# First expert pair in a row, the ranks' order ahead of it, and weight units on a 512-byte start

## The chip, the core and the metric

The kernel runs on one core of a Trainium2 chip. The metric is the device time of one execution in microseconds (us), the median of several runs. The core has a matrix engine (TensorE, PE in the rows), a vector engine (VectorE, DVE), a scalar engine (ScalarE, ACT), GpSimd (POOL) and SyncE (SP), which here issues nearly all transfers from HBM into the on-chip memory (SBUF). Sixteen DMA engines carry each transfer out. Matrix products land in PSUM banks, of which this kernel uses four as `mm` and four as `ax`.

## The reference

One layer of a backbone over 256 tokens of 1,024 features: an attention and gating part, and then a mixture of experts. All of it is in float32.

```python
x = layer_norm(ALPHA * x + g1 * mix_x, ln1_g, ln1_b)
logits = t @ router_w + router_b                 # t: modulated layer norm of x, 256 x 1024
top_vals, top_idx = lax.top_k(logits, 4)         # 4 of 32 experts for each token
combine = sum(one_hot(top_idx, 32) * softmax(top_vals))
for each expert e:
    gu = t @ w_gu[e] + b_gu[e]                   # 1024 x 2048
    gate, lin = minimum(gu[:, :1024], 7), clip(gu[:, 1024:], -7, 7)
    y = ((lin + 1) * gate * sigmoid(1.702 * gate)) @ w_down[e] + b_down[e]
    acc += combine[:, e] * y
x = layer_norm(ALPHA * x + g2 * acc, ln2_g, ln2_b)
```

An expert's weights are 12 MiB, all 32 together 384 MiB.

## The kernel before

**Units and the stream.** SBUF is cut into 26 units of 8 KiB in each of the 128 partitions (1 MiB each, pool `uni`). Weights come as pieces that fill one unit (L193 to L232): 38 for the front part, then per expert 8 for gate and up and 4 for down. `pump` issues the next piece of the list into a free unit, and `done` frees a unit after its last product and pumps one piece more. The code is recorded by hand in the order in which each engine runs it; SP's queue is in order too, so a transfer that waits for its unit holds back those behind it.

**Groups.** The first group is the fixed pair of experts 0 and 1, whose pieces can be issued early. Then come twelve groups of one, two or four experts, sorted by how many tokens each expert got: counting tokens (`rank_counts`) gives ranks and the permutation `perm`, `rank_order` turns it into the list of expert numbers `ordi`, and SP loads a number from it (L213) before it can issue that expert's first piece. So no piece of the second group can be issued before `ordi` is written; `streams` puts all those pieces on the list.

**One group** (`group`, L1199): four steps of gate and up (gate 0, up 0, gate 1, up 1; two halves each, the bias first, L894, then L1114), with the activation on VectorE and ScalarE between, a transpose of the result (`h_T`, L1145), and two down products (L1160). Between them, at named places ("in0" inside the first step, "gu0" behind it, and so on), hooks run other work on the same engines. For the first pair these are the counts (in0), the order, the tables by rank and the stream (gu0), the tables' lookup (in1), `finish_G`, the first weighting transpose and the next group's one-hot tables (gu1), and the next group's gather (gu2: L888 and the weighting transpose L951). Two units are taken from the pair's freed ones for other use: `take_late` after the first step (table and bias storage, with four small loads, L997), `t2_unit` after the third.

**Before the pair** the second half of the tokens is routed (L795 to L804), its one-hot table written (L875) and gathered (L888) into the banks `gb0`; `modulate_cols` (L776) scales the gathered columns, the first half on VectorE, the second on ScalarE, and `gate` computes the four weights per token.

Of the kernel before, what the change touches and what calls it, by code (L numbers as in the profile page):

```python
# [18 lines left out]
P = 128  # L19
# [5 lines left out]
NE = 32  # L25
# [40 lines left out]
def hybrid_layer_kernel(  # L66
# [12 lines left out]
    router_w = router_w[0]  # L79
    w_gu, b_gu, w_dn, b_dn = exp_w_gu, exp_b_gu[0], exp_w_down, exp_b_down[0]  # L80

    cst = ctx.enter_context(tc.tile_pool(name="cst", bufs=1))
    uni = ctx.enter_context(tc.tile_pool(name="uni", bufs=1))
    mo = ctx.enter_context(tc.tile_pool(name="mo", bufs=2))
    sm = ctx.enter_context(tc.tile_pool(name="sm", bufs=4))
    pm = ctx.enter_context(tc.tile_pool(name="pm", bufs=4, space=bass.MemoryType.PSUM))
# [72 lines left out]
        return bass.AP(tensor=src.tensor, offset=src.offset, ap=[[0, parts], [1, n]])  # L159


    ident = cst.tile([P, P], F32, name="ident")
    make_identity(nc, ident)
    mhalf = cst.tile([P, 1], F32, name="mhalf")
    G.memset(mhalf, -0.5)


# [604 lines left out]
        for j in range(4):  # L772
            G.partition_broadcast(late_v["g2"][:, j * 256:(j + 1) * 256], late["rows"][32 * j:32 * j + 1, :])

    def modulate_cols(dst, bank, hh, act_only=False):
        for k in range(4):  # L776
            kk = hh * 4 + k
            src = bank[:, k * P:(k + 1) * P]
            if act_only or hh:
                S.activation(dst[:, kk, :], src, AF.Identity, scale=sc2[:, kk:kk + 1], bias=sh2[:, kk:kk + 1])  # L780
            else:
                V.tensor_scalar(dst[:, kk, :], src, sc2[:, kk:kk + 1], sh2[:, kk:kk + 1],
                                op0=ALU.mult, op1=ALU.add)
# [32 lines left out]
    def route_T(t, hh):  # L816
        tT = late["xg"][:, t * 1024:t * 1024 + 1024].rearrange("p (k n) -> p k n", n=P)
        pt = ax_bank()
        for k in range(4):
            PE.transpose(pt[:, k * P:(k + 1) * P], late["tMv"][:, t, (hh * 4 + k) * P:(hh * 4 + k + 1) * P], ident)  # L820
        return lambda: modulate_cols(tT, pt, hh, t == 0)

    def route_mm(t):
        tT = late["xg"][:, t * 1024:t * 1024 + 1024].rearrange("p (k n) -> p k n", n=P)
# [66 lines left out]
    def gu_bias(part, j, sel):  # L891
# [2 lines left out]
        PE.matmul(b, sel[r, :], bgu[r, :], start=True, stop=False)  # L894
        return b

    oh0 = mo.tile([P, TT, 2, 64], F32, tag="oh", bufs=1, name="oh0")
    gb0 = [mm_bank() for _ in range(2)]
    ln_second(0)
# [21 lines left out]
    top(1)  # L921
    choose(1)
    positions(1)
    one_hot(oh0, pm1[:, :, 0:2], 1)
    for hh in range(2):
        gather_mm(gb0[hh], oh0, 1, hh)
    tM, xg_u = late["tMv"], late["xg"]
    for u in (late["l1"], gg_u):
        release(u)
# [28 lines left out]
    def gather(oh, banks=None):  # L958
        xg_i[0] ^= 1
        xg = xg_u[:, xg_i[0] * 1024:xg_i[0] * 1024 + 1024].rearrange("p (k n) -> p k n", k=KT)  # L960
        for hh in range(2):
            if banks:
                b = banks[hh]
            else:
                b = ax_bank()
                for t in range(TT):
                    gather_mm(b, oh, t, hh)
            modulate_cols(xg, b, hh)
        return xg

    xg0 = gather(oh0, gb0)
    msk4 = mo.tile([P, TT, P], F32, tag="sT", name="msk4").rearrange("p t n -> p (t n)")[:, 0:P].bitcast(BF16)
    msk4 = msk4.rearrange("p (t r e) -> p t r e", t=TT, r=4)
    V.tensor_copy(msk4, mskb[:, :, None, :].to_broadcast([P, TT, 4, NE]))
    for t in range(TT):
        gate(t)
    cur = [xg0, None]
    ohg0 = weigh(oh0, comb[:, :, 0:2])


    cc = cst.tile([P, 1], F32, name="cc")
    kr = cst.tile([P, NE], F32, name="kr")
    kc = cst.tile([P, 1], F32, name="kc")
    rank = cst.tile([P, 1], F32, name="rank")
    perm = cst.tile([P, NE], F32, name="perm")
    ordi = cst.tile([1, NE], I32, name="ordi")

    late_v = {}

# [14 lines left out]
                          start=True, stop=True)  # L1004
        V.tensor_copy(dst, b[:, 0:2 * TT * NE].rearrange("p (a t e) -> p a t e", a=2, t=TT))

    pc4 = t2_own[1].rearrange("p (a t r e) -> p a t r e", a=2, t=TT, r=4)
    V.tensor_copy(pc4[:, 0], pm1[:, :, None, :].to_broadcast([P, TT, 4, NE]))
    V.tensor_copy(pc4[:, 1], comb[:, :, None, :].to_broadcast([P, TT, 4, NE]))

    def rank_counts():
        b = ax_bank()
        for t in range(TT):
            PE.matmul(b[:, 0:NE], ones_b, mskb[:, t, :], start=t == 0, stop=t == TT - 1)
        for t in range(TT):
            PE.matmul(b[:, 64:65], msk4[:, t].rearrange("p r e -> p (r e)"), ones_b[:, 0:1],
                      start=t == 0, stop=t == TT - 1)
        V.tensor_copy(cc, b[:, 64:65])
        V.scalar_tensor_tensor(kr, b[:, 0:NE], 32.0, keyb, op0=ALU.mult, op1=ALU.add)
        V.scalar_tensor_tensor(kc, cc, 32.0, keyc, op0=ALU.mult, op1=ALU.add)  # L1020
        V.tensor_scalar(kr, kr, kc, None, op0=ALU.is_gt)
        V.reduce_sum(rank, kr, axis=AX.X)
        V.tensor_scalar(perm, iota0[:, 0:NE], rank, None, op0=ALU.is_equal)

    def rank_order():
        b = ax_bank()
        PE.matmul(b[0:1, 0:NE], ecol, perm[0:NE, :], start=True, stop=True)
        V.tensor_copy(ordi, b[0:1, 0:NE])
        b = ax_bank()
        for a in range(2):  # L1030
            for t in range(TT):
                PE.transpose(b[:, (a * TT + t) * P:(a * TT + t + 1) * P],
                             pc4[:, a, t].rearrange("p r e -> p (r e)"), ident)
        V.tensor_copy(late_v["pcT"], b.rearrange("p (a n) -> p a n", a=2))
# [70 lines left out]
    def gu_step(n, gid, part, j, xg, sel, between=None):  # L1105
        w = P // n
        b = gu_first.pop(0) if gu_first else gu_bias(part, j, sel)
        for half in range(2):
            if half and between:
                between()  # L1110
            first = gid == 0 and part == j == half == 0
            for a, k in ([(a, k) for a in range(n) for k in range(4)] if first else
                         [(a, k) for k in range(4) for a in range(n)]):
                PE.matmul(b[a * w:(a + 1) * w, :], xg[:, half * 4 + k, a * w:(a + 1) * w],  # L1114
                          weights((gid, part, j, half, a))[:, k, :], start=False, stop=half == 1 and k == 3)
                if first and k == 3:
                    done((gid, part, j, half, a))
            if not first:
                for a in range(n):
                    done((gid, part, j, half, a), (gid, part, half, a) != (0, 0, 1, 1))  # L1120
        if (gid, part) == (0, 0):
            (t2_unit if j else take_late)()
        return b

    def swiglu_gate(b):
# [64 lines left out]
    def group(n, gid, cur, sel, hooks):  # L1190
        xg = cur[0]

        def hook(name):
            for f in hooks.get(name, ()):
                f()

        b = gu_step(n, gid, 0, 0, xg, sel, lambda: hook("in0"))
        if gid == 0:
            hook("gu0")  # L1199
        g_0 = swiglu_gate(b)  # L1200
        if gid != 0:
            hook("gu0")
        b = gu_step(n, gid, 1, 0, xg, sel, lambda: hook("in1"))
        l_0 = swiglu_lin(b, g_0)
        hook("gu1")
        b = gu_step(n, gid, 0, 1, xg, sel, lambda: hook("in2"))
        g_1 = swiglu_gate(b)
        h0 = h_T(l_0)
        hook("gu2")
        b = gu_step(n, gid, 1, 1, xg, sel, lambda: hook("in3"))  # L1210
        l_1 = swiglu_lin(b, g_1)
        yb = [mm_bank() for _ in range(2)]
        if gid == len(groups) - 1:
            hs = (h0, h_T(l_1))
            zst2.extend(sm.tile([P, 2, 6], F32, tag="zst", bufs=2, name=nm("zst")) for _ in range(TT))
            down(n, gid, hs, 0, yb[0], last=True)
            ys = [scaled(yb[0], 0)]
            scatter(ys, cur[1], [0])
            down(n, gid, hs, 1, yb[1], last=True)
            y = scaled(yb[1], 1)  # L1220
            for t in range(TT):
                PE.matmul(sums[t], cur[1][:, t, :], y, start=False, stop=True)
                V.bn_stats(zst2[t][:, 1, :], sums[t])
            return None
        hs = [h0]
        down(n, gid, hs, 0, yb[0], 0, 4)
        hs.append(h_T(l_1))
        down(n, gid, hs, 0, yb[0], 4)
        ys = [scaled(yb[0], 0)]
        down(n, gid, hs, 1, yb[1])  # L1230
        for h in hs:
            t2_free(h)
        ys.append(scaled(yb[1], 1))
        return lambda: scatter(ys, cur[1])

    plan = list(PLAN)
# [26 lines left out]
    for gi, rk in enumerate(groups):  # L1263
        n = 2 if rk is None else len(rk)
        nxt = groups[gi + 1] if gi + 1 < len(groups) else None
        box = {}
        hooks = {k: [] for k in ("in0", "gu0", "in1", "gu1", "in2", "gu2", "in3")}

        def prep():
            a, m = nxt[0], len(nxt)  # L1270
# [14 lines left out]
            cur[1] = weigh_T(ohg0)  # L1285

        if gi == 0:
            hooks["in0"] += [rank_counts]
            hooks["gu0"] += [rank_order, streams]
            hooks["gu1"] += [finish_G]  # L1290
            hooks["in1"] += [lambda: by_rank(late_v["pcr"], perm[0:NE, :])]
            hooks["gu1"] += [first_T, prep]
        else:
            if nxt:
                hooks["gu0"] += [prep]
# [10 lines left out]
            S.dma_start(l2_u[0:1, 0:D], ln2_g)  # L1306
            S.dma_start(l2_u[0:1, D:2 * D], ln2_b)
        if nxt:
            hooks["gu2"] += [fetch]
        if gi == 4:  # L1310
            def spread(js):
                for j in js:
# [104 lines left out]
```

## Time and profile before

| | us |
|---|---|
| median of 3 runs | 1139.0 |
| lowest, highest | 1137.99, 1139.81 |
| the profiled execution's own time | 1136.04 |
| its span (first to last instruction) | 1134.3 |
| TensorE busy | 997.4 (88%) |
| VectorE busy | 306.0 (27%) |
| DMA queue of SP: share of 16 engines | 96.4% |

The span begins with the front part; the first expert pair runs from about 198 to 252 us, and the twelve other groups fill the rest. A busy TensorE is not one at its peak: its products are pipelined. The 450 MB that SP's queue moves are nearly all weights. A row of stretches gives busy times, the granted TensorE clock (1.00 is the upper level, 2.4 GHz) and the rate in GB/s; a timeline row gives a start, a duration, what ran, and in brackets how long the engine had been idle and what ended that.

### The profile page before, as it was taken

The numbers are of one execution on the slowest core, as the hardware profiler recorded it, in microseconds if no ns is written. First come the engines' busy times: TensorE is split into PE (matmuls) and PEld (weight loads), VectorE is DVE, ScalarE is ACT, GpSimd is POOL, SyncE is SP. The second block draws the span as 40 slices with busy tenths as digits, with TensorE's granted clock in tenths as the row PEclk, the third lists the DMA queues.
The fourth block names the chain that finished last, engine by engine and source line by source line (L and its number), as shares of the span: only waits on it lengthen the run. The fifth ranks groups of instructions, "written<-read, shape, count | busy, mean of one in ns | idle before, by whom it ended". The sixth has DMA issues, their size and how long they took to land. (4 is left out here: it accounts for less than half of the span.)

```text
span 1134.3 us, 13253 instructions
## 1 busy us (share of the span) xinstructions
PE 997.4 (88%) x5140; PEld 421.6 (37%) x5140; DVE 306.0 (27%) x621; ACT 132.8 (12%) x286; POOL 27.7 (2%) x57
## 2 busy tenths in 40 slices
PE   5999897999779999986799999987799999977765
PEld 4897465333214433321253434222134343421111
DVE  6596765314103121210121212111021211201003
ACT  4343342100100101110010101000001010100000
POOL 2000300000000000000000000000000000000000
PEclk9999898999989999988999999988899999999988
DMA  9998599799999999999989999999999999999995
GB/s 381 421 396 325 229 360 366 307 386 422 420 421 421 421 420 421 422 420 421 420 343 422 421 421 420 421 422 421 421 422 420 420 422 420 421 422 421 421 420 190
DMA packets 66296, 451.32 MB, mean 398 GB/s; under 512 B 8627, under 2 KB 8883, under 8 KB 12725
## 3 DMA queue, kind: packets, MB, share of 16 engines
q1 hardware_dynamic: 66082, 450.03, 96.4%
q8 instruction: 42, 0.69, 0.2%
q10 hardware_dynamic: 148, 0.40, 0.1%
q14 instruction: 24, 0.20, 0.0%
HBM read 449.36 MB, written 1.05 MB: 397 GB/s over the span
## 5 line engine op out<-in xcount | busy, mean ns | idle before, releaser
L1114 PE MATMUL mm<-w,xg 128*32 128x512 f32 (+2 forms) x2048 | 424.9, 620 | 42.7 <-DMA w<-in_exp_w_gu_dram 42.7
L1160 PE MATMUL mm<-w,t 128*32 128x512 f32 (+2 forms) x1024 | 235.2, 645 | 52.2 <-DMA w<-in_exp_w_down_dram 43.6
L1114 PEld LDWEIGHTS mm<-w,xg 128*32 128x32 f32 (+2 forms) x2048 | 127.9, 130 | 325.6 <-issue 242.4
L1160 PEld LDWEIGHTS mm<-w,t 128*32 128x32 f32 (+2 forms) x1024 | 67.4, 133 | 207.9 <-issue 109.9
L1187 DVE TENSOR_TENSOR t<-mm,late 128x512 f32<-128x512 f32 x26 | 18.0, 692 | 263.0 <-PE mm L1160 263.0
L1130 ACT ACTIVATE t<-t 128x512 f32<-128x512 f32 x26 | 16.4, 630 | 583.0 <-DVE t L1128 583.0
L1137 DVE TENSOR_SCALAR t<-mm 128x512 f32<-128x512 f32 x26 | 18.0, 692 | 222.7 <-PE mm L1114 222.7
L1128 DVE TENSOR_SCALAR t<-mm 128x512 f32<-128x512 f32 x26 | 18.0, 691 | 215.4 <-PE mm L1114 215.4
L894 PE MATMUL mm<-bgu,sel 32*128 32x512 f32 x104 | 58.4, 641 | 4.0 <-PEq L1240 4.0
L1170 PE MATMUL ax<-t,sT 128*128 128x512 f32 x100 | 46.3, 605 | 0.8 <-DVE t L1187 0.8
L888 PE MATMUL ax<-oh,tM 128*128 128x128 f32 x384 | 44.8, 275 | 0.0
L888 PEld LDWEIGHTS ax<-oh,tM 128*128 128x128 f32 x384 | 43.8, 192 | 0.0
L1149 ACT COPY t<-ax 128x512 f32<-128x512 f32 x26 | 15.0, 576 | 190.6 <-PE ax L1145 190.6
L245 POOL TENSOR_TENSOR rs<-rs,mhalf 128x1 f32<-128x1 f32 x12 | 9.5, 797 | 1047.4 <-DVE mv L257 919.5
L1172 DVE TENSOR_TENSOR xin<-xin,ax 128x512 f32<-128x512 f32 x50 | 33.2, 684 | 5.2 <-PE ax L1170 4.8
L1170 PEld LDWEIGHTS ax<-t,sT 128*128 128x128 f32 x100 | 18.0, 189 | 29.2 <-issue 24.6
L894 PEld LDWEIGHTS mm<-bgu,sel 32*128 32x128 f32 x104 | 15.3, 183 | 34.3 <-issue 24.5
L780 ACT ACTIVATE xg<-ax,sh,sc 128x128 f32<-128x128 f32 x60 | 22.4, 457 | 32.3 <-PE ax L888 26.5
L414 DVE TENSOR_TENSOR wlo<-w,whi 128x1024 fp32r<-128x1024 f32 x20 | 23.7, 1223 | 3.1 <-ACT whi L411 3.1
L411 ACT CAST whi<-w 128x1024 fp32r<-128x1024 f32 x20 | 20.1, 1047 | 9.5 <-PE mm L446 9.5
L1145 PEld LDWEIGHTS ax<-ident,t 128*128 128x128 f32 x104 | 11.2, 141 | 21.8 <-issue 16.8
L525 DVE SCALAR_TENSOR_TENSOR accB<-w,front,accB 128x2048 f32<-128x2048 f32 x8 | 18.8, 2348 | 0.0
(261 smaller groups left out, 717.8 us busy)
## 6 DMA issues: line engine op xcount, KB each, us to landing
w<-in_exp_w_gu_dram SPq DMA_DIRECT2D x256, 1024.0 KB, 19.8
w<-in_exp_w_down_dram SPq DMA_DIRECT2D x124, 1024.0 KB, 19.8
w<-in_w_front_dram SPq DMA_DIRECT2D x38, 1024.0 KB, 10.7
w<-in_exp_w_down_dram SPq DMA_DIRECT2D x4, 512.0 KB, 16.1
w<-in_exp_w_down_dram SPq DMA_DIRECT2D x8, 256.0 KB, 6.9
T<-in_rpb_dram SPq DMA_DIRECT2D x2, 768.0 KB
xin<-in_x_dram SPq DMA_DIRECT2D x2, 512.0 KB
cin<-in_ctx_dram SPq DMA_DIRECT2D x2, 512.0 KB, 6.4
```

What stands on the lines that cost most here:

```text
L411: S.copy(av[:, k], w[:, k])
L414: V.tensor_tensor(bv[:, k], w[:, k], av[:, k].bitcast(F32), op=ALU.subtract)
L525: V.scalar_tensor_tensor(accB_u, w[:, 0, :], sT[:, k, 0:1], accB_u, op0=ALU.mult, op1=ALU.add)
L780: S.activation(dst[:, kk, :], src, AF.Identity, scale=sc2[:, kk:kk + 1], bias=sh2[:, kk:kk + 1])
L888: PE.matmul(bank[:, k * P:(k + 1) * P], late["tMv"][:, t, (hh * 4 + k) * P:(hh * 4 + k + 1) * P], oh[:, t].rearrange("p n w -> p (n w)"), ...
L894: PE.matmul(b, sel[r, :], bgu[r, :], start=True, stop=False)
L1114: PE.matmul(b[a * w:(a + 1) * w, :], xg[:, half * 4 + k, a * w:(a + 1) * w], weights((gid, part, j, half, a))[:, k, :], start=False, stop= ...
L1128: V.tensor_scalar_min(gtile, b, 7.0)
L1137: V.tensor_scalar(lt, b, 7.0, -7.0, op0=ALU.min, op1=ALU.max)
L1160: PE.matmul(bank[a * w:(a + 1) * w, :], hs[kk // 4][:, kk % 4 * P + a * w:kk % 4 * P + (a + 1) * w], weights((gid, nn, r0, a))[:, k, :], s ...
L1170: PE.matmul(b, st[:, t, :], ys[nn], start=True, stop=True)
L1172: V.tensor_tensor(sl, sl, b, op=ALU.add)
```

## The change

It does four things.

- A new pool `pad` with one tile of 128 bytes stands first, and the units' pool `uni` in front of the constants' pool `cst`. In the built program the units begin at byte 512 of each partition instead of 9,888. All else about them is the same.
- `rank_counts` is split. Its products stand ahead of the second half of the gather before the pair, its VectorE steps (`rank_perm`) behind that gather, and ScalarE modulates the first half of those columns, VectorE the second.
- `rank_order` is split too. The part that gives `ordi`, and the stream, move to the hook "in0" inside the first step. The tables by rank become `ranks_T`.
- Three hooks are added in the down part of a group: "dn0" inside the first down product, "dn1" between the two, "dn2" behind the second. In the first pair all the other work moves there, and `take_late` goes to the end of the fourth step.

```diff
+    pad = ctx.enter_context(tc.tile_pool(name="pad", bufs=1))
+    uni = ctx.enter_context(tc.tile_pool(name="uni", bufs=1))
     cst = ctx.enter_context(tc.tile_pool(name="cst", bufs=1))
-    uni = ctx.enter_context(tc.tile_pool(name="uni", bufs=1))
...
+    mhalf = pad.tile([P, 32], F32, name="mhalf")[:, 0:1]
...
-    mhalf = cst.tile([P, 1], F32, name="mhalf")
...
+    def rank_counts():
+        msk4 = mo.tile([P, TT, P], F32, tag="sT", name="msk4").rearrange("p t n -> p (t n)")[:, 0:P].bitcast(BF16)
+        msk4 = msk4.rearrange("p (t r e) -> p t r e", t=TT, r=4)
+        V.tensor_copy(msk4, mskb[:, :, None, :].to_broadcast([P, TT, 4, NE]))
+        b = ax_bank()
+        for t in range(TT):
+            PE.matmul(b[:, 0:NE], ones_b, mskb[:, t, :], start=t == 0, stop=t == TT - 1)
+        for t in range(TT):
+            PE.matmul(b[:, 64:65], msk4[:, t].rearrange("p r e -> p (r e)"), ones_b[:, 0:1],
+                      start=t == 0, stop=t == TT - 1)
+        return b
+
+    def rank_perm(b):
+        V.tensor_copy(cc, b[:, 64:65])
+        V.scalar_tensor_tensor(kr, b[:, 0:NE], 32.0, keyb, op0=ALU.mult, op1=ALU.add)
+        V.scalar_tensor_tensor(kc, cc, 32.0, keyc, op0=ALU.mult, op1=ALU.add)
+        V.tensor_scalar(kr, kr, kc, None, op0=ALU.is_gt)
+        V.reduce_sum(rank, kr, axis=AX.X)
+        V.tensor_scalar(perm, iota0[:, 0:NE], rank, None, op0=ALU.is_equal)
...
     positions(1)
+    counts = rank_counts()
     one_hot(oh0, pm1[:, :, 0:2], 1)
     for hh in range(2):
         gather_mm(gb0[hh], oh0, 1, hh)
+    rank_perm(counts)
...
-            modulate_cols(xg, b, hh)
+            modulate_cols(xg, b, hh, not hh if banks else None)
...
     def rank_order():
         b = ax_bank()
         PE.matmul(b[0:1, 0:NE], ecol, perm[0:NE, :], start=True, stop=True)
         V.tensor_copy(ordi, b[0:1, 0:NE])
+
+    def ranks_T():
+        pc4 = t2("pc4").rearrange("p (a t r e) -> p a t r e", a=2, t=TT, r=4)
+        V.tensor_copy(pc4[:, 0], pm1[:, :, None, :].to_broadcast([P, TT, 4, NE]))
+        V.tensor_copy(pc4[:, 1], comb[:, :, None, :].to_broadcast([P, TT, 4, NE]))
         b = ax_bank()
...
-                    done((gid, part, j, half, a), (gid, part, half, a) != (0, 0, 1, 1))
-        if (gid, part) == (0, 0):
-            (t2_unit if j else take_late)()
+                    done((gid, part, j, half, a), (gid, j, half, a) != (0, 1, 1, 1))
+        if (gid, j) == (0, 1):
+            (take_late if part else t2_unit)()
...
         down(n, gid, hs, 0, yb[0], 0, 4)
         hs.append(h_T(l_1))
+        hook("dn0")
         down(n, gid, hs, 0, yb[0], 4)
         ys = [scaled(yb[0], 0)]
+        hook("dn1")
         down(n, gid, hs, 1, yb[1])
...
         ys.append(scaled(yb[1], 1))
+        hook("dn2")
...
-            hooks["in0"] += [rank_counts]
-            hooks["gu0"] += [rank_order, streams]
-            hooks["gu1"] += [finish_G]
-            hooks["in1"] += [lambda: by_rank(late_v["pcr"], perm[0:NE, :])]
-            hooks["gu1"] += [first_T, prep]
+            hooks["in0"] += [rank_order, streams]
+            hooks["dn0"] += [finish_G, ranks_T]
+            hooks["dn1"] += [lambda: by_rank(late_v["pcr"], perm[0:NE, :]), prep]
+            hooks["dn2"] += [first_T]
...
-            hooks["gu2"] += [fetch]
+            hooks["gu2" if gi else "dn2"] += [fetch]
```

TensorE, first step of the pair, before: the last half of the gather (L888), the first half of the step for either expert (L1114), the counts (L1014, L1016), two of the eight products of the second half, the order (L1027) and the tables' transposes (L1032).

```order
L888 MATMUL mm_1601<-oh_1599,tM_1473 128x128 x4
L1114 MATMUL mm_1685<-w_1117,xg_1474 64x512 x4
L1114 MATMUL mm_1685<-w_1214,xg_1474 64x512 x4
...
L1014 MATMUL ax_1829<-mskb,one_b 128x32
...
L1016 MATMUL ax_1829<-one_b,msk_1791 128x1
L1114 MATMUL mm_1685<-w_1224,xg_1474 64x512
L1114 MATMUL mm_1685<-w_1285,xg_1474 64x512
...
L1027 MATMUL ax_1853<-perm,ecol 1x32
L1032 MATMUL ax_1856<-ident,t_1_76 128x128 x4
```

The same place after:

```order
L912 MATMUL ax_1779<-mskb,one_b 128x32
...
L914 MATMUL ax_1779<-one_b,msk_1777 128x1
L890 MATMUL mm_1609<-oh_1608,tM_1476 128x128 x4
L890 MATMUL mm_1610<-oh_1608,tM_1476 128x128 x4
L1122 MATMUL mm_1694<-w_1120,xg_1477 64x512 x4
L1122 MATMUL mm_1694<-w_1217,xg_1477 64x512 x4
L1030 MATMUL ax_1841<-perm,ecol 1x32
L1122 MATMUL mm_1694<-w_1227,xg_1477 64x512
L1122 MATMUL mm_1694<-w_1288,xg_1477 64x512
```

The counts stand ahead of the gather, the order behind the first half of the step, and the tables' transposes are gone from here.

SP, the queue behind the pair's last piece, before: that piece, the four loads of `take_late`, the first expert number and its first piece.

```order
L225 DMA w_1823<-in_exp_w_down_dram 128x2048
L997 DMA late_1848<-in_exp_b_down_dram 32x256 x4
L213 TENSOR_LOAD ordi
L213 ISA x2
L218 ISA
L218 DMA w_1862<-in_exp_w_gu_dram 128x2048
```

After:

```order
L227 DMA w_1835<-in_exp_w_down_dram 128x2048
L215 TENSOR_LOAD ordi
L215 ISA x2
L220 ISA
L220 DMA w_1844<-in_exp_w_gu_dram 128x2048
```

The number is loaded straight behind the last piece; the four small loads stand thirteen pieces further on.

TensorE, from the fourth step's bias to the second group's first bias, after (before, the gather L888, its weighting transpose L951 and the tables' lookup stood ahead of the fourth step):

```order
L896 MATMUL mm_1957<-bgu,sel_1600 128x512
...
L1153 MATMUL ax_2002<-ident,t_249_1947 128x128 x4
L1040 MATMUL ax_2014<-ident,t_1_79 128x128 x4
...
L1024 MATMUL ax_2033<-perm,late_1981 128x32 x4
...
L982 MATMUL ax_2072<-ident,ohg_1825 128x128 x2
L890 MATMUL ax_2077<-oh_2039,tM_1476 128x128 x8
L890 MATMUL ax_2090<-oh_2039,tM_1476 128x128 x8
L982 MATMUL ax_2103<-ident,ohg_2044 128x128 x2
L896 MATMUL mm_2108<-bgu,sel_2042 128x512
```

What stood between the steps now stands between and behind the down products.

## Rows read from the trace of the kernel before

**Rows 1.** Page, costliest groups: busy us, mean ns, idle before it, releaser.

```profile
L1160 PE MATMUL mm<-w,t 128*32 128x512 f32 (+2 forms) x1024 | 235.2, 645 | 52.2 <-DMA w<-in_exp_w_down_dram 43.6
```

**Rows 2.** Stretches: us; PE, PEld, DVE, ACT, POOL busy; clock, DMA share, GB/s.

```profile
200.00:245.00 45.00, 44.33 (x221) 17.97 (x221) 13.60 (x39) 6.21 (x15) 1.82 (x4) 1.00 0.81 327
...
300.00:560.00 260.00, 224.28 (x1016) 79.14 (x1015) 42.47 (x95) 15.18 (x32) 0.00 (x0) 0.95 1.01 421
```

**Rows 3.** The same view in short stretches, around the two holes.

```profile
209.00:210.00 1.00, 1.00 (x8) 0.35 (x6) 0.56 (x1) 0.36 (x1) 0.00 (x0) 1.00 0.35 49
210.00:211.00 1.00, 1.00 (x8) 0.36 (x6) 0.00 (x0) 0.99 (x2) 0.00 (x0) 1.00 0.47 115
211.00:212.00 1.00, 1.00 (x7) 0.25 (x3) 0.41 (x1) 0.56 (x1) 0.00 (x0) 1.00 0.94 393
230.00:235.00 5.00, 5.00 (x25) 1.66 (x26) 0.00 (x0) 0.81 (x3) 0.00 (x0) 1.00 0.71 267
235.00:240.00 5.00, 5.00 (x26) 1.70 (x24) 1.39 (x2) 0.00 (x0) 0.00 (x0) 1.00 0.89 369
```

**Rows 4.** Timeline of SP's queue, 197 to 210 us: start, duration, transfer.

```profile
201.99 0.33 SPq L225 DMA_DIRECT2D w<-in_exp_w_down_dram  x1
...
203.76 1.72 SPq L997 DMA_DIRECT2D late<-in_exp_b_down_dram  x4
...
208.92 0.38 SPq L218 DMA_DIRECT2D w<-in_exp_w_gu_dram  x1
```

**Rows 5.** Timeline of TensorE in the first pair: start, duration, products.

```profile
203.67 0.21 PE L1014 MATMUL ax<-mskb,one_b 128*128 128x32 bf16 x2
...
207.44 0.21 PE L1027 MATMUL ax<-perm,ecol 32*1 32x32 f32 x2
207.58 0.66 PE L1032 MATMUL ax<-ident,t 128*128 128x128 f32 x4
...
216.34 0.44 PE L951 MATMUL ax<-ident,ohg 128*128 128x128 f32 x2
...
225.27 3.74 PE L888 MATMUL ax<-oh,tM 128*128 128x128 f32 x32
228.84 0.38 PE L951 MATMUL ax<-ident,ohg 128*128 128x128 f32 x2
...
240.66 0.66 PE L1145 MATMUL ax<-ident,t 128*128 128x128 f32 x4
241.99 10.52 PE L1160 MATMUL mm<-w,t 128*64 128x512 f32 x48 [0.67 <-ACT t L1149]
252.44 1.12 PE L894 MATMUL mm<-bgu,sel 32*128 32x512 f32 x2
253.49 3.64 PE L1114 MATMUL mm<-w,xg 128*32 128x512 f32 x32
```

**Rows 6.** Timeline of VectorE, 198 to 208 us: the copy, first and last rank step, cast.

```profile
198.81 0.22 DVE L974 COPY msk<-mskb 128x256 bf16<-128x256 bf16 x1
...
203.96 0.16 DVE L1018 COPY cc<-ax 128x1 f32<-128x1 f32 x1 [0.18 <-PE ax L1016]
...
205.15 0.59 DVE L1023 TENSOR_SCALAR perm<-iotas,rank 128x32 f32<-128x32 f32 x1
207.69 0.18 DVE L1028 CAST ordi<-ax 1x32 int32<-1x32 f32 x1 [1.95 <-PE ax L1027]
```

**Rows 7.** DMA queues, 62.8 to 63.4 us (two lines), then 300 to 560 us.

```profile
DMA packets 269, 0.10 MB, mean 163 GB/s; under 512 B 258, under 2 KB 258, under 8 KB 262
...
q1 hardware_dynamic: 269, 0.10, 61.4%
...
DMA packets 15029, 109.50 MB, mean 421 GB/s; under 512 B 1672, under 2 KB 1672, under 8 KB 1674
...
q1 hardware_dynamic: 15010, 109.29, 101.2%
```

More of the change, by code (lines that the diff above doesn't have):

```diff
@@ L773, in finish_G, with modulate_cols @@
             G.partition_broadcast(late_v["g2"][:, j * 256:(j + 1) * 256], late["rows"][32 * j:32 * j + 1, :])
-    def modulate_cols(dst, bank, hh, act_only=False):
+    def modulate_cols(dst, bank, hh, act_only=None):
         for k in range(4):
@@ L778, in modulate_cols @@
             src = bank[:, k * P:(k + 1) * P]
-            if act_only or hh:
+            if act_only if act_only is not None else hh:
                 S.activation(dst[:, kk, :], src, AF.Identity, scale=sc2[:, kk:kk + 1], bias=sh2[:, kk:kk + 1])
@@ L820, in route_T @@
             PE.transpose(pt[:, k * P:(k + 1) * P], late["tMv"][:, t, (hh * 4 + k) * P:(hh * 4 + k + 1) * P], ident)
-        return lambda: modulate_cols(tT, pt, hh, t == 0)
+        return lambda: modulate_cols(tT, pt, hh, True if t == 0 else None)
     def route_mm(t):
@@ L895, in gu_bias @@
         return b
+    cc = cst.tile([P, 1], F32, name="cc")
+    kr = cst.tile([P, NE], F32, name="kr")
+    kc = cst.tile([P, 1], F32, name="kc")
+    rank = cst.tile([P, 1], F32, name="rank")
+    perm = cst.tile([P, NE], F32, name="perm")
+    ordi = cst.tile([1, NE], I32, name="ordi")
+    def rank_counts():
[16 more added lines that the diff above has]
+        V.tensor_scalar(perm, iota0[:, 0:NE], rank, None, op0=ALU.is_equal)
     oh0 = mo.tile([P, TT, 2, 64], F32, tag="oh", bufs=1, name="oh0")
@@ L967, in gather @@
                     gather_mm(b, oh, t, hh)
-            modulate_cols(xg, b, hh)
+            modulate_cols(xg, b, hh, not hh if banks else None)
         return xg
     xg0 = gather(oh0, gb0)
-    msk4 = mo.tile([P, TT, P], F32, tag="sT", name="msk4").rearrange("p t n -> p (t n)")[:, 0:P].bitcast(BF16)
-    msk4 = msk4.rearrange("p (t r e) -> p t r e", t=TT, r=4)
-    V.tensor_copy(msk4, mskb[:, :, None, :].to_broadcast([P, TT, 4, NE]))
     for t in range(TT):
@@ L978, in hybrid_layer_kernel @@
     ohg0 = weigh(oh0, comb[:, :, 0:2])
[L981 to L986, printed above, removed]
     late_v = {}
@@ L1005, in by_rank @@
         V.tensor_copy(dst, b[:, 0:2 * TT * NE].rearrange("p (a t e) -> p a t e", a=2, t=TT))
[L1007 to L1023, printed above, removed]
     def rank_order():
@@ L1266, in hybrid_layer_kernel @@
         box = {}
-        hooks = {k: [] for k in ("in0", "gu0", "in1", "gu1", "in2", "gu2", "in3")}
+        hooks = {k: [] for k in ("in0", "gu0", "in1", "gu1", "in2", "gu2", "in3", "dn0", "dn1", "dn2")}
         def prep():
```

## The prediction

> **What bounds the kernel now.** I read the costliest groups first. The expert matmuls of the down product stood idle 52.2 us, 43.6 of them for weights from HBM [rows 1]: the engine that multiplies waits for the transfers, one piece at a time. Then the stretches: from 300 to 560 us the 16 DMA engines move 421 GB/s and are never idle [rows 2]. A piece of 1 MiB (one weight unit) takes 1.0486 MB / 421 GB/s = 2.49 us there. So from about 300 us on the end is set by one thing: how many bytes are left, which the change doesn't touch, and how long the DMA engines have stood still before. I therefore look for stretches below 421. From 200 to 245 us the rate is 327 [rows 2]: 45 x (1 - 327/421) = **10.0 us of standstill**, in the middle of the first expert pair. Two holes make it up: 230 to 240 us loses 5 x (1 - 267/421) + 5 x (1 - 369/421) = 2.45 us [rows 3], and the rest, 7.6 us, lies before 212.
>
> The queue of SP tells why. The last piece of the first pair is issued at 201.99, as soon as TensorE has freed a unit, and the next piece of weights only at 208.92 [rows 4]. Which experts come next is read from the tile `ordi`, and its cast on VectorE ends at 207.69 + 0.18 = 207.87 [rows 6]. The number then has to be loaded by SP (208.92 - 207.87 = 1.05 us). After the issue the stream needs time to reach its rate: 49 + 115 + 393 kB by 212 [rows 3] are 1.32 us of full rate, so it is as if it had started at 210.68, 1.76 us after the issue. The second hole is one of free units: TensorE runs the gather of the next group (225.27 to 229.2) and other small work between the products of the first pair [rows 5], and a unit is free for loading only when its product is done; one more unit goes to `t2_unit`.
>
> **The change, part by part.** I rebuild the first pair on TensorE and the transfers behind it.
>
> 1. *Ranks ahead.* The four count matmuls (0.21 us at 203.67 [rows 5]) now stand in front of the second half of the first gather, behind a VectorE copy (0.22 us at 198.81 [rows 6]). They are on the path to the first expert product. They overlap in part: bounds 0.2 and 0.4, I take +0.3 us. The six VectorE steps that make `perm` (203.96 to 205.15 + 0.59 = 205.74, 1.8 us [rows 6]) now run beside the gather and the first product; to pay for that ScalarE modulates the first half of the gathered columns and VectorE the second, which is first read at the second half of the product, over 5 us later: nothing.
>
> 2. *Order ahead.* The matmul of `rank_order` moves from behind the first gate step to its middle, where the counts stood. That half ended at 203.67, now 203.97. Cast 0.43 us after the matmul's start (207.44 to 207.87 [rows 5, 6]): 204.4. VectorE's own queue is the other bound: it was through with everything ahead of the ranks at 203.78 (203.96 less 0.18 idle [rows 6]); with 1.8 us more in front, and at most that, the cast ends at 205.7 at the latest. Two table copies leave that queue and a wait for ScalarE falls away, so I take 204.5, near the early end. Issue at 204.5 + 1.05 = 205.5, full rate as from 207.3 in place of 210.68: **3.4 us earlier**. The three other expert numbers each cost SP another 1.05 us, which passes while it waits for units.
>
> 3. *No other work inside the steps.* The end of the pair's products was 252.44 [rows 5]. Taken out before it: the counts 0.2, the weighting transpose 0.4 (216.34), the next gather with its weighting 3.9 (225.27 to 229.15), and the tables' transposes 0.6 (207.58), which go into the wait for ScalarE between 240.66 and 241.99 and so are covered. New end: 252.44 + 0.3 - 5.1 = 247.6. Pieces: 24 units come free in the pair, one takes its last piece, `t2_unit` and `take_late` take two, so 21 pieces of the next group can be issued. The tightest places are the two steps that give a unit away: ten pieces end at 207.3 + 24.9 = 232.2, and the next two units are free by about 228 (203.97, the order's 0.2, six half steps of 3.6, two biases of 1.05 and a transpose of 0.5). A refill needs 1.76 us of lead. It has it, so the second hole closes: **2.45 us**.
>
> 4. *`take_late` later.* Its four loads (issued at 203.76 [rows 4], 128 KiB together, 0.31 us at 421) fell into the standstill; now they stand in a busy stretch: **-0.3 us**. SP gets to them when the fourth step ends; the unit behind them in the queue comes free later anyway.
>
> 5. *Gather behind the down steps.* It has no cover on TensorE now: 247.6 + 0.4 + 3.9 + 1.05 for the bias (252.44 to 253.49) = 253.0 for the next group's first product, against 253.49 before [rows 5]. So TensorE is there no later. The 21 pieces last until 207.3 + 21 x 2.49 + 0.3 = 259.9; the first half of that product (3.64 us [rows 5]) frees units at 256.6, and 258.1 would do. Margin 1.5 us: nothing.
>
> 6. *Aligned units.* The unit pool began at byte 9,888 of a partition and begins at 512. Every weight row is 8,192 B, so before each started 160 bytes past a multiple of 256. No row of the trace has units at another address, so bounds: from 300 to 560 us an 8 KiB packet takes 313.6 ns (101.2% of 16 x 260 us, less 1,672 small ones at 13 ns, over 13,355 packets) and from 62.8 to 63.4 us, where the router's rows of 128 B pass, a small one takes about 13 ns (61.4% of 9.6 us less seven 8 KiB packets, four of 2 KiB, over 258) [rows 7]. Solved for a price per byte and one per packet: 8.2 ns per packet, 2.6% of a big row. That is the most that a better start can give back; the least is nothing. The 128 B rows start at either of two places against the 256-byte grid, some crossing it and some not, and carry the same 8 ns: it looks like a price of a packet, not of its place. I take 0.
>
> *A rule against that:* the Trainium skill (DMA: Bandwidth & Descriptors, How a descriptor splits into AXI transactions) says that a transfer that doesn't begin on a 256-byte boundary starts at the boundary below and pays for the unused bytes in 32-byte beats. By it a row costs 261 beats and not 256; an estimate from that page is 1.9%, or 17 us over the 896 us of weights below, and the time would be 1116. Its table speaks of fetching; here the crooked end is the one written.
>
> **Sum.** 3.4 + 2.45 - 0.3 + 0 = 5.55, less 0.1 for what the first hole gets longer: 5.4 us. From the profiled execution's own time, 1136.04 (span 1134.3): 1130.6. The median of the runs is 1139.0, 2.96 above it: **1133.6**. What is gained by 260 us arrives at the end whole, because from about there on TensorE is the one that waits [rows 1, 2].
>
> **Rivals.**
> - *The start of a row is what its 8.2 ns are paid for.* 360 pieces come after 207 us, 360 x 2.49 = 896 us, times 2.6% = 23 us more: **1110**. For it: 421 GB/s is flat whatever the engines do. Against it: the small packets.
> - *The hole moves and doesn't close.* If the cast comes at the late bound (-1.2) and units run short in the steps that give one away, part of the 2.45 stays: 5.4 - 1.2 - 1.7 = 2.5, **1136.5**. For it: units come in twos, so a lead of under 1.76 us is soon lost. Against it: four us of slack at 228.
> - *Slower: TensorE is late at the next group.* Gather, modulation and bias follow the last down product in a chain. If a stall there lets the granted clock fall from its upper level, 2.4 GHz (1.00 in the rows from 209 to 240 [rows 3]), to 1.2, as it does somewhere between 300 and 560, where TensorE waits for weights (mean 0.95 [rows 2]), then bias, two half steps and the accumulator's start (about 1 + 3.6 + 1.1 + 3.6) take twice as long: 9.4 - 1.5 of margin = 7.9 us of new standstill, net +2.5: **1141.5**. It decides from 1.5 us of delay on. Against it: the stall, if there is one, is one modulation long.
>
> **How the numbers follow.** Forecast 0.70 (its own range 1131 to 1136: cast 204.4 to 205.7, the second hole closed or nearly); aligned rows pay 0.09; the hole moves 0.14; slower 0.07. A measurement of this kernel can tell 0.2%, 2.3 us, from no change. Faster: 0.70 + 0.09 + 0.03 of the third = 0.82; same 0.13; slower 0.05. For 8 in 10 the forecast's range is stretched up to 1138, most of the third case, and down to 1124, for a small part of the 2.6%.
>
> **What would show it.** The first load of the next group's weights issued near 205.5 and not 208.9; GB/s near 421 in every stretch from 208 to 300; `take_late`'s loads near 231; the next group's first product near 253; the rate from 300 to 560 still 421. A rate of 425 or more there would show that the rows' start counts, and that step 6 is wrong; a new hole near 260 that step 5 is; a first issue past 206.5 that step 2 is.

## The result, and the profile after

| | before | after |
|---|---|---|
| median, us | 1138.49 | 1120.93 |
| lowest, highest | 1135.40, 1139.81 | 1120.46, 1126.17 |
| the profiled execution's own time | 1136.04 | 1120.84 |
| its span | 1134.3 | 1119.1 |

The ratio is 0.986, with an interval of 0.9825 to 0.9896: 17.6 us less; before has one execution more here than in its first table. Measured again later, the changed kernel came to 1119.03 us, 0.984 of before [0.982, 0.986]. The forecast was 1133.6, its range 1124 to 1138: the sign was right, the size a third of what came, and the time lies below the range.

The down products still wait for weights, a little less than in [rows 1]. Page of after, costliest groups: busy us, mean ns of one | idle before it, and what ended most of it.

```profile
L1168 PE MATMUL mm<-w,t 128*32 128x512 f32 (+2 forms) x1024 | 233.1, 642 | 47.5 <-DMA w<-in_exp_w_down_dram 39.1
```

The stretches of after that answer to [rows 2] and to the last two of [rows 3] (us; PE, PEld, DVE, ACT and POOL busy; clock, DMA share, GB/s):

```profile
200.00:245.00 45.00, 44.76 (x207) 16.32 (x207) 13.57 (x35) 5.71 (x13) 2.35 (x4) 1.00 0.93 378
300.00:560.00 260.00, 229.97 (x1025) 81.42 (x1025) 42.50 (x95) 15.20 (x32) 0.00 (x0) 0.93 1.01 427
...
230.00:235.00 5.00, 5.00 (x26) 1.61 (x24) 1.04 (x2) 0.00 (x0) 0.89 (x3) 1.00 1.01 426
235.00:240.00 5.00, 4.76 (x28) 2.00 (x26) 2.29 (x4) 0.59 (x1) 1.46 (x3) 1.00 1.01 426
```

Two things are new. From 200 to 245 us the rate is 378 and not 327 GB/s, and the hole from 230 to 240 is gone: that is the order, as forecast. And from 300 to 560 the rate is 427 where it was 421. The new order touches only the first pair, which is over by then, and a rate of 425 or more there is the sign that the prediction had named for its step 6 being wrong.

SP's queue in after, 204 to 242 us (start, duration, transfer, how many in the row; compare [rows 4]):

```profile
204.79 0.33 SPq L227 DMA_DIRECT2D w<-in_exp_w_down_dram  x1
207.97 26.24 SPq L220 DMA_DIRECT2D w<-in_exp_w_gu_dram  x13
234.33 1.96 SPq L1018 DMA_DIRECT2D late<-in_exp_b_down_dram  x4
237.31 1.77 SPq L220 DMA_DIRECT2D w<-in_exp_w_gu_dram  x2
```

From the pair's last piece to the next group's first it takes 207.97 - 204.79 = 3.18 us, before 208.92 - 201.99 = 6.93 [rows 4]: 3.75 us saved, 3.4 forecast. The times stand 2.4 to 3.3 us later than forecast, because in this execution the front part ended 2.8 us later (204.79 against 201.99). So absolute times of two profiles don't compare here. I measure instead from the issue of the pair's last piece to the end of the span, and call it the *rest*: 1134.3 - 201.99 = 932.3 us before, 1119.1 - 204.79 = 914.3 after, 18.0 us less. The *rest* comes from one profile of each kernel, and it can't see what lies ahead of that piece.

VectorE and TensorE in after (start, duration, what, idle before): the cast of the list, the first and the last down products, the next group's gather, bias and first product.

```profile
206.72 0.18 DVE L1031 CAST ordi<-ax 1x32 int32<-1x32 f32 x1 [0.46 <-PE ax L1030]
```

```profile
233.68 3.60 PE L1168 MATMUL mm<-w,t 128*64 128x512 f32 x16
...
243.13 7.09 PE L1168 MATMUL mm<-w,t 128*64 128x512 f32 x32
250.15 0.44 PE L982 MATMUL ax<-ident,ohg 128*128 128x128 f32 x2
250.43 3.74 PE L890 MATMUL ax<-oh,tM 128*128 128x128 f32 x32
254.00 0.38 PE L982 MATMUL ax<-ident,ohg 128*128 128x128 f32 x2
254.31 1.12 PE L896 MATMUL mm<-bgu,sel 32*128 32x512 f32 x2
255.36 3.64 PE L1122 MATMUL mm<-w,xg 128*32 128x512 f32 x32
```

The gather stands behind the down products with nothing to cover it, as step 5 said, and the next group's first product comes 255.36 - 204.79 = 50.6 us behind the last piece, 253.49 - 201.99 = 51.5 before. Where the forecast had a margin of 1.5 us, no hole opened:

```profile
258.00:261.00 3.00, 3.00 (x32) 1.20 (x28) 0.80 (x2) 0.00 (x0) 0.00 (x0) 1.00 1.01 429
261.00:264.00 3.00, 3.00 (x32) 0.95 (x25) 2.02 (x4) 0.00 (x0) 0.00 (x0) 1.00 1.02 431
```

DMA queues of after, 300 to 560 us, the lines that answer to the second pair of [rows 7]:

```profile
DMA packets 15224, 110.91 MB, mean 427 GB/s; under 512 B 1694, under 2 KB 1694, under 8 KB 1696
...
q1 hardware_dynamic: 15206, 110.71, 100.9%
```

The sum of step 6, with these: 100.9% of 16 x 260 us, less 1,694 x 13 ns, over 15,224 - 1,696 = 13,528 packets is 308.7 ns for an 8 KiB row, before 313.6. The DMA engines are as busy as ever; each row takes 4.9 ns less. The trace also keeps every packet's own time, and it says the same: in after 13,492 of 13,519 such rows took 309 ns (mean 309.5), in before 99 in 100 took 309 to 322 (mean 314.3).

### The profile page after: what moved, and what is told of

Read it like the earlier page. It is cut to its first block, busy times and chain, and to the rows that moved or that the text cites. A ratio compares the mean times of both kernels' runs of the same rounds, so it can differ in the third digit from the quotient of the medians.

```text
span 1119.1 us, 13259 instructions
## 1 busy us (share of the span) xinstructions
PE 993.3 (89%) x5140; PEld 423.2 (38%) x5140; DVE 306.5 (27%) x621; ACT 133.1 (12%) x286; POOL 28.3 (3%) x57
## 5 line engine op out<-in xcount | busy, mean ns | idle before, releaser
L1122 PE MATMUL mm<-w,xg 128*32 128x512 f32 (+2 forms) x2048 | 419.7, 622 | 36.0 <-DMA w<-in_exp_w_gu_dram 36.0
```

## The experiments

The theory after the first profile: the start of the units gives back some 12 us over the whole stream, the order 5 or 6 us within the first pair. Rivals: the rate rose through the new order, or through the lower place of the units and not their start; and, inside the order, the two holes are not two separate losses.

### Which of the two changes

Only the start, in the order of before (units at 512), and only the order, with the units at 416, which is 160 past a multiple of 256, as before:

```diff
+    pad = ctx.enter_context(tc.tile_pool(name="pad", bufs=1))
+    uni = ctx.enter_context(tc.tile_pool(name="uni", bufs=1))
     cst = ctx.enter_context(tc.tile_pool(name="cst", bufs=1))
-    uni = ctx.enter_context(tc.tile_pool(name="uni", bufs=1))
...
-    mhalf = cst.tile([P, 1], F32, name="mhalf")
+    mhalf = pad.tile([P, 32], F32, name="mhalf")[:, 0:1]
```

> The kernel before with the units on byte 512 and nothing else (the order of work is the old one). If the start of the units pays for the rest of the gain: 427 GB/s in the stretches from 300 to 560 us in place of 421, and 11 to 14 us less than before, about 1126. If the order of the first pair pays for all of it: 421 GB/s and no change.

```diff
-    mhalf = pad.tile([P, 32], F32, name="mhalf")[:, 0:1]
+    mhalf = pad.tile([P, 8], F32, name="mhalf")[:, 0:1]
```

> The changed kernel with its first tile cut to 32 bytes, so that the units begin at byte 416, which is 160 past a multiple of 256 as in the kernel before. The prediction's own sum for the order alone: 5 to 6 us less than before, 421 GB/s from 300 to 560 us. If the order pays for all: about 1121.

The start alone: 1124.53 us, 0.9899 [0.9849, 0.995]. The order alone: 1132.63, 0.9956 [0.9936, 0.9976], 5.0 us less than the kernel before, measured beside it. Stretches of the first, then of the second:

```profile
300.00:560.00 260.00, 225.07 (x1022) 80.01 (x1022) 42.48 (x95) 15.20 (x32) 0.00 (x0) 0.95 1.01 426
```

```profile
300.00:560.00 260.00, 224.11 (x1015) 79.03 (x1015) 42.48 (x95) 15.20 (x32) 0.00 (x0) 0.95 1.01 421
```

The rate follows the start, not the order. From 200 to 245 us it is the other way round: 326 GB/s with the start alone, 375 with the order alone. By the medians the start gives 13.1 us and the order 5.0, 18.1 together against 17.6 for the whole change; by the *rest* 12.2 + 5.4 = 17.6 against 18.0. Within that scatter the two add up to the whole.

### Which starts

Two more starts in the new order (448 and 384: 192 and 128 past a multiple of 256), then two further ones at both ends (480 and 544: 224 and 32 past one), and, in the order of before, the first multiple of 256 above the old place, which is none of 512:

```diff
-    mhalf = pad.tile([P, 32], F32, name="mhalf")[:, 0:1]
+    mhalf = pad.tile([P, 16], F32, name="mhalf")[:, 0:1]      # units at 448
...
+    mhalf = cst.tile([P, 8], F32, name="mhalf")[:, 0:1]       # no pad: 384
...
+    mhalf = pad.tile([P, 24], F32, name="mhalf")[:, 0:1]      # 480
...
+    mhalf = pad.tile([P, 40], F32, name="mhalf")[:, 0:1]      # 544
...
-    mhalf = cst.tile([P, 1], F32, name="mhalf")               # before
+    mhalf = cst.tile([P, 32], F32, name="mhalf")[:, 0:1]      # 9,984
```

> The changed kernel with the units at byte 448: a multiple of 64, not of 128. If a start on a multiple of 64 is enough, 427 GB/s and about 1121, as the changed kernel; if 256 or 512 is needed, 421 GB/s and about 1133, as with 416.

> The changed kernel with the units at byte 384: a multiple of 128, not of 256. If 64 or 128 is enough, 427 GB/s and about 1121; if rows have to start on a multiple of 256, as a rule of whole 256-byte transactions would have it, 421 GB/s and about 1133.

> The kernel before in its own order, with nothing but 128 bytes of room in place of 4 for the tile mhalf, so that the units begin at byte 9,984 of a partition (a multiple of 256, not of 512) in place of 9,888. Theory A, a start on a multiple of 256 is what counts: 427 GB/s from 300 to 560 us and 1124 to 1126 us, as with the units at 512 in this order. Theory B, it takes a multiple of 512, or the low place of the units rather than their start: 421 GB/s and 1136 to 1139 us.

> The changed kernel with 96 bytes in place of 128 in front of the units, which then begin 224 bytes past a multiple of 256 (starts 128, 160 and 192 past one gave 421 GB/s and 1132.6 to 1133.6 us). Theory A, any start that is not on a multiple of 256 costs the same: 421 GB/s from 300 to 560 us and 1132 to 1134 us. Theory B, the price grows with the bytes between the boundary below and the start: 224/160 of 1.4% is 2.0%, 418 to 419 GB/s and 1138 to 1139 us.

> The changed kernel with 160 bytes in front of the units, which then begin 32 bytes past a multiple of 256 (two one-column tiles share one, so that it fits). Theory A, any start that is not on a multiple of 256 costs the same: 421 GB/s from 300 to 560 us and 1132 to 1134 us. Theory B, the price grows with the bytes between the boundary below and the start: 32/160 of 1.4% is 0.3%, 425 to 426 GB/s and 1123 to 1124 us.

| units at | past a multiple of 256 | order | GB/s, 300 to 560 us | median us | ratio | *rest* us |
|---|---|---|---|---|---|---|
| 512 | 0 | new | 427 | 1120.93 | 0.986 [0.9825, 0.9896] | 914.3 |
| 544 | 32 | new | 419 | 1135.16 | 0.9985 [0.9969, 1.0001] | 930.3 |
| 384 | 128 | new | 421 | 1133.14 | 0.9961 [0.9942, 0.9981] | 926.9 |
| 416 | 160 | new | 421 | 1132.63 | 0.9956 [0.9936, 0.9976] | 926.9 |
| 448 | 192 | new | 421 | 1133.56 | 0.9956 [0.994, 0.9971] | 927.0 |
| 480 | 224 | new | 419 | 1135.24 | 0.9982 [0.9967, 0.9997] | 930.9 |
| 512 | 0 | old | 426 | 1124.53 | 0.9899 [0.9849, 0.995] | 920.1 |
| 9,984 | 0 | old | 427 | 1126.47 | 0.9897 [0.9882, 0.9912] | 920.7 |

The kernels were measured in four groups, each beside the kernel before, whose median lay between 1136.89 and 1138.49; so the ratios and the *rest* compare more closely than the medians.

The rows of 9,984, and of 544:

```profile
300.00:560.00 260.00, 222.87 (x1016) 78.17 (x1015) 43.88 (x97) 15.18 (x32) 0.00 (x0) 0.95 1.01 427
```

```profile
300.00:560.00 260.00, 218.84 (x1016) 78.80 (x1017) 42.51 (x95) 15.20 (x32) 0.00 (x0) 0.99 1.01 419
```

A multiple of 256 is enough, high or low in SBUF, so the lower place of the units isn't what pays. A multiple of 128 is not. And the price doesn't grow with the distance: 32 bytes past the boundary cost no less than 160. Of the expectations for 480 and 544, theory B had the rate right at 480 (419, though its time was 3 us too long), and falls at 544, where it wanted 425 to 426 GB/s and 1123 to 1124 us. Theory A isn't exact either: 32 and 224 cost more than 128 to 192, 3.3 to 4.0 us by the *rest* and 315.0 to 315.2 ns a row against 314.0 to 314.3. Those two are the starts 32 bytes from the nearest boundary; why they cost more wasn't tried.

### Which part of the order

With the units at 512: the list ahead without the down steps' hooks (`take_late`, `t2_unit`, `fetch` and the copies for the tables go back to their places of before too), and these hooks with the list where it was (there the two halves of the columns go back to their engines of before too).

```diff
-            hooks["dn0"] += [finish_G, ranks_T]
-            hooks["dn1"] += [lambda: by_rank(late_v["pcr"], perm[0:NE, :]), prep]
-            hooks["dn2"] += [first_T]
+            hooks["gu0"] += [ranks_T]
+            hooks["gu1"] += [finish_G]
+            hooks["in1"] += [lambda: by_rank(late_v["pcr"], perm[0:NE, :])]
+            hooks["gu1"] += [first_T, prep]
```

> Units at 512 as in the changed kernel; of the new order only the ranks and the list of experts come ahead, while finish_G, the tables, the next gather and the two units given away stay at their places of before. Theory A, the two holes are two separate losses: the first one shrinks by 3.4 us, the second (14 us from 228 at 364 GB/s with units at 512 in the old order) stays, and the time is 1124.5 - 3.4 = 1121. Theory B, a stream that starts earlier only comes earlier to the place where units run short: the second hole grows by what the first one lost, the stretch from 228 to 242 falls under 330 GB/s, and the time is 1123.5 to 1125.

```diff
-    counts = rank_counts()
...
-    rank_perm(counts)
...
-            hooks["in0"] += [rank_order, streams]
+            hooks["in0"] += [lambda: rank_perm(rank_counts())]
+            hooks["gu0"] += [rank_order, streams]
```

> Units at 512 as in the changed kernel; of the new order only the work of the first pair goes to the down steps and the two units are given away later, while the counts stand inside the first step and the list of experts behind it, as before. Theory A, the two holes are two separate losses: the first load of the next group is issued about 209 as before, the stretch from 228 to 242 goes to 426 GB/s, and the time is 1124.5 - 2.5 = 1122. Theory B, without the earlier list the units never run short of anything that matters there: 1124 to 1125, although the second hole is gone.

The list alone: 1125.75 us, 0.9915 [0.9891, 0.994]. The hooks alone: 1125.0, 0.989 [0.9873, 0.9908]. The start alone had 0.9899 and 0.9897: by the times neither half brings anything that can be told from nothing. The *rest* tells more: 920.1 and 920.7 for the start alone (units at 512, at 9,984), 920.7 with the list ahead, 918.2 with the hooks, 914.3 with both; profiles of the same order and start differ by up to 0.6. So the hooks alone are worth about 2 us, the list alone nothing, both together 6. For the list alone theory B came true, the stretch from 228 to 242 included, with the time 0.8 us above its range. With the hooks alone the time is theory B's, but the next group's first load comes 6.95 us behind the pair's last piece, as before, and the second hole closes, as theory A said; by the *rest* this is worth 1.9 to 2.5 us, about the 2.45 that the prediction had put on that hole:

```profile
228.00:242.00 14.00, 13.76 (x70) 4.94 (x66) 3.33 (x5) 0.59 (x1) 2.35 (x4) 1.00 1.01 427
```

SP's queue and three stretches with the list ahead alone show why that half brings nothing:

```profile
202.31 0.33 SPq L227 DMA_DIRECT2D w<-in_exp_w_down_dram  x1
205.47 2.67 SPq L220 DMA_DIRECT2D w<-in_exp_w_gu_dram  x2
208.25 1.82 SPq L1018 DMA_DIRECT2D late<-in_exp_b_down_dram  x4
211.97 29.82 SPq L220 DMA_DIRECT2D w<-in_exp_w_gu_dram  x13
```

```profile
206.00:212.00 6.00, 6.00 (x31) 1.93 (x28) 1.54 (x3) 1.91 (x2) 1.80 (x4) 1.00 0.95 362
212.00:228.00 16.00, 16.00 (x88) 7.70 (x89) 5.05 (x13) 1.48 (x3) 0.00 (x0) 1.00 0.98 363
228.00:242.00 14.00, 13.44 (x67) 5.21 (x65) 2.14 (x5) 2.29 (x6) 0.00 (x0) 1.00 0.77 315
```

The same stretches with the start alone:

```profile
206.00:212.00 6.00, 6.00 (x32) 1.99 (x28) 1.73 (x4) 1.83 (x2) 0.22 (x1) 1.00 0.45 135
212.00:228.00 16.00, 16.00 (x86) 7.43 (x85) 4.92 (x12) 1.56 (x4) 0.00 (x0) 1.00 0.99 402
228.00:242.00 14.00, 13.83 (x70) 5.57 (x68) 2.52 (x6) 1.90 (x6) 0.00 (x0) 1.00 0.90 364
```

The list came 3.8 us earlier and the first hole closed (362 against 135). Then two units are issued, the four small loads, and the next piece only at 211.97: from there the stream is short of units, 363 against 402 and 315 against 364. From 206 to 242 as a whole the two kernels move the same, 344 and 343 GB/s:

```profile
206.00:242.00 36.00, 35.44 (x182) 14.83 (x178) 8.73 (x19) 5.67 (x11) 1.80 (x4) 1.00 0.89 344
```

```profile
206.00:242.00 36.00, 35.83 (x184) 15.00 (x180) 9.17 (x21) 5.29 (x11) 0.22 (x1) 1.00 0.86 343
```

SP's queue in the kernel with the list ahead, 204 to 242 us, line, what it waited for, total, times, longest: it waits 1.8 us for the list, and 22.2 for products of the steps to hand back their units. With the start alone the same window has 2.4 for the list and 20.6 for such products.

```profile
SPq L220 <- PE mm L1123: 22.2, 7, 8.5
...
SPq L215 <- DVE ordi L1031: 1.8, 1, 1.8
```

With both halves, in after, the same 36 us move 407:

```profile
206.00:242.00 36.00, 35.76 (x164) 11.91 (x162) 7.92 (x14) 3.60 (x5) 2.35 (x4) 1.00 0.99 407
```

By 242 us TensorE has handed back as many units, whenever the list came. An earlier list only moves the standstill from the first hole to the second; it pays when the units come sooner too, and that is what the hooks do.

### The list ahead of the pair

In after, the ranks' permutation is ready before the pair's first product. So the list can be made there, and its number be loaded while SP waits for the pair's last piece:

```diff
     rank_perm(counts)
+    rank_order()
...
-            hooks["in0"] += [rank_order, streams]
+            hooks["in0"] += [streams]
```

> The changed kernel with one step more: the matmul and cast that give the list of experts stand ahead of the first product of the pair, right behind the ranks' steps. The list is then ready while SP still waits for the unit of the pair's last piece, and the number is loaded in that wait. Theory A, the list is what the first load waits for: 3.2 us between the pair's last piece and the next one become 1.9 to 2.1, and the time is 1120.9 - 1.2 = 1119.7. Theory B, a unit is what it waits for, and the number's load counts for nothing: the 3.2 us stay and so does the time, 1120.5 to 1121.5.

SP's queue:

```profile
203.77 0.33 SPq L227 DMA_DIRECT2D w<-in_exp_w_down_dram  x1
205.55 27.35 SPq L220 DMA_DIRECT2D w<-in_exp_w_gu_dram  x13
```

The 3.18 us became 1.78, and the median 1119.19, 0.9837 [0.9823, 0.9851]: it looked like the 1.2 us of theory A, but the time of after was from another group of runs. So both ran again on one chip:

> The changed kernel once more, beside the version with the list of experts ahead of the first product, on one chip. Both theories: 1120 to 1122 us, since it is the same kernel. From the issue of the pair's last piece to the end of the span it should be 914 to 915 us, as in its first profile, wherever the front part ends in this execution.

> The version with the list of experts ahead of the first product once more, beside the changed kernel on one chip. Theory A, the 1.4 us by which the first load comes earlier behind the pair's last piece are kept to the end: 1.2 to 1.7 us under the changed kernel of this call. Theory B, units run short later and take most of it back, as where the list alone was moved: under 0.6 us.

After 1119.03 (0.984 [0.982, 0.986]; 1120 to 1122 was expected), the new version 1119.91 (0.9852 [0.983, 0.9874]). The *rest* is 914.3 and 914.4 for after, 913.8 and 913.4 for the new version: of 1.4 us, 0.5 to 1.0 is left at the end. But the list's matmul now stands ahead of the pair, where the *rest* doesn't see it: from TensorE's last routing product (L843) to the pair's last piece it takes 8.86 us in both profiles of after, 9.00 and 9.05 in the new version. That leaves 0.3 to 0.8 us, which the times can't tell. The profiles lean to theory B; a version that beats the changed kernel measurably it is not.

## Why the prediction was wrong, step by step

*Steps 2 and 3, the sum of the order: right.* 5.4 us were forecast; the order with a bad start is 5.0 us by the medians and 932.3 - 926.9 = 5.4 by the *rest* (926.9 to 927.0 in the three kernels at 384, 416 and 448). First issue, closed second hole and the next group's first product all came as written, counted from the last piece. What was wrong is the split: 3.4 for the list and 2.45 for the hole stand there as two losses that can be won one by one. Alone they are worth about 0 and 2; the list is worth its 3.4 (3.8 by the *rest*) only where the hooks have been moved. The mechanism is that of the second rival (the hole moves), which I had taken for an accident of the whole and not for what the first half does by itself.

*Step 1: too dear by 0.3 us.* From the last routing product (L841 before, L843 after) to the first expert product it takes 198.31 - 193.15 = 5.16 us before and 201.11 - 195.93 = 5.18 after: the counts fall into the wait for the one-hot table. *Steps 4 and 5: as forecast.* `take_late` issued 234.33 - 204.79 = 29.5 us behind the last piece, forecast 231 - 201.99 = 29.0; its 128 packets of 1 KiB pass from 241.7 to 243.6 and take 0.37 us of the 16 engines, forecast 0.3; no hole near 260. The third rival, slower by a fallen clock at the next group, didn't come: the clock is 1.00 from 258 to 261.

*Step 6: the step that failed.* It put the term for aligned rows at nothing where 1.4% came: 427 against 421 GB/s, 4.8 or 4.9 ns of an 8 KiB row. Over the 896 us that it had counted this is 12.6 us. The measured price is 11.6 to 12.2 us in the old order and 12.6 in the new by the *rest*, 11.8 and 13.1 by the medians of the old order. With it the sum would have been 1133.6 - 12.6 = 1121.0.

The wrong turn was to read from the router's rows of 128 B what an 8 KiB row can pay for its start. The observation was right: the trace has 1,152 packets of 128 B, and they took 13.1 ns in before and 12.9 in after, although the router's table lies in a unit, so that its rows' starts moved too. But the long rows did pay. Solved again for after, with 12.9 and 309.5 ns, the step's two equations give 8.2 ns a packet, where the packet records of before (13.1 and 314.3) give 8.3; what fell is the price per byte, from 37.4 to 36.8 ps. So what a bad start cost wasn't in the 8.2 ns at all, and 2.6% was no bound on it: that 1.4% lay between 0 and 2.6% is luck, and the 1110 of the first rival priced the right idea by the wrong term. That short rows carry no such price is no reason to put it at nothing for long ones; 0.09 for "aligned rows pay" was far too little. A smaller slip: the small packets from 300 to 560 us are of 4 B and take 9 ns, not 13, which moves the row by half a nanosecond.

The rule of the Trainium skill that the prediction had put beside the sum (DMA: Bandwidth & Descriptors, How a descriptor splits into AXI transactions) gave 1.9% and 1116. It was nearer than my 0. Its count of unused bytes before the start doesn't hold here: by it 32 bytes past the boundary would cost a fifth of 160, and they cost 419 against 421 GB/s. What would fit better is the other half of the rule, that transactions start on 256-byte boundaries: by an estimate from it an 8 KiB row off the boundary takes 33 of them and not 32, wherever it starts. No run here separates that from other causes, and it doesn't say why 32 and 224 cost more than 128 to 192; why the price is nearly flat stays open.

## What to carry to other kernels

Where a long stream of large rows bounds a kernel, put the buffers it lands in on a multiple of 256 bytes within the partition: 1.4 to 1.9% of the stream's time hung on that here, with rows of 8 KiB, and one pool opened in another place did it. Where a transfer waits for two things, a number and a free buffer, bringing one of them forward can move the wait to the other; price the two together. Here the number alone brought nothing, the buffers alone 2 us, both 6. And where two ends of a bound are far apart and no row separates them, an experiment on a copy of the kernel is cheaper than an argument by the nearest row.

## What the runs showed that I had not expected

The front part ends at another time in each profile, and this goes with the clock granted in its first 28 us. Five profiles with 1.00 there issue the pair's last piece at 200.99 to 202.51, four with 0.94 at 202.70 to 203.77, five with 0.88 at 204.42 to 205.05, across kernels of either order and start. Before, then after:

```profile
0.00:28.00 28.00, 13.97 (x119) 11.22 (x120) 17.65 (x37) 12.04 (x17) 7.33 (x40) 1.00 0.95 381
```

```profile
0.00:28.00 28.00, 13.48 (x107) 11.00 (x108) 15.82 (x36) 12.14 (x17) 7.36 (x40) 0.88 0.92 376
```

1.00 is the upper level, 2.4 GHz; a mean of 0.88 means that the lower, 1.2 GHz, was granted for part of it. Some 2.7 us between the means of the first and the last group are as much as the order's single terms, and more than the 2.3 us that a measurement of this kernel was taken to tell from nothing. That the clock makes the difference, and isn't only a sign of it, wasn't tried.
